# A two-layer convolution and retention decoder on one core: input blocks in the order v, gate, conv, q, k, merge gates, and matmuls kept in written order

## The chip, the cores and the metric

The kernel runs on 1 core of one Trainium2 chip. The metric is the device time of one execution in microseconds (us), as the median of several runs. The core has a matrix engine (TensorE, "PE" in the profile, with its weight loads as "PEld"), a vector engine (VectorE, DVE), an activation engine (ScalarE, ACT), GpSimd (POOL) and SyncE (SP), which issues most of the transfers. Each engine works through its own instructions strictly in order and waits for others by semaphores.

## The reference

Two layers over 256 tokens of 1024 channels, in float32. Cut to what matters:

```python
def hybrid_layer(x, ...):
    h = rmsnorm(x, norm_mix)
    cb, cc, cu, q, k, v, g, ga, gb = jnp.split(h @ w_in, split_points, axis=-1)
    y_conv = (cb * causal_conv3(cc * cu, conv_w)) @ w_conv_out
    o = retention(rotary(q), rotary(k), v)       # 4 heads, decayed scores, then values
    o = (o - mean(o)) * rsqrt(var(o) + EPS) * ret_norm   # per head, over 256 value channels
    y_ret = (silu(g) * o) @ w_ret_out
    x = x + (sigmoid(ga) * y_conv + sigmoid(gb) * y_ret) @ w_o
    h2 = rmsnorm(x, norm_mlp)
    return x + square(relu(h2 @ w_up)) @ w_down

def reference(x, ...):
    for i in range(2):
        x = hybrid_layer(x, ...)
    return rmsnorm(x, norm_final)
```

## The kernel before

Channels lie on the 128 partitions and tokens on the free axis, as 8 tiles of 128 channels by 256 tokens. All weights come as 152 blocks of 1024 input by 256 output channels (1 MB each), read once, in the order of use. A block is loaded by SP into one of three `raw` buffers. `split_block` then makes from it two float32r tiles in one of three `parts` buffers: ACT casts the high part (L99), DVE subtracts to get the low part (L100), each in two instructions of 128x1024. Activations are split the same way. `proj` multiplies one block with 32 matmuls: for each of the 8 input tiles and 2 output halves one of 512 columns (high weights times high and low activations together) and one of 256 columns (low weights). `collect` adds the two sums in PSUM (ACT copy, DVE add).

A layer goes through the 32 blocks of the input projection in the order of `IN_ORDER`, then `yc` times `w_conv_out` (4 blocks), `yr` times `w_ret_out` (4), the merged `mg` times `w_o` (4), then the MLP (16 up, 16 down). The very first block is multiplied straight in float32 (`whole_tokens`), since no split is ready.

Work that doesn't belong to one block is queued with `later(n, fn)`: `fn` is emitted after the matmuls of the n-th block from there, that of the block about to begin being the first. This holds the norm factors (`factors`: Newton steps for `rr`), the rotation tables, the score products (`scores`), the value products (`mix_values`), and the head normalisation in two halves i = 0, 1 of two heads: `head_sums(i)` sums the squares over channels with two matmuls into `var_ps`, DVE writes the variance and ACT its square root to `rm`; `head_out(i)` takes a DVE reciprocal, one Newton step (`newton`: three DVE operations), scales `sg` (gate times values) with four DVE operations and splits it into the parts of `yr`, one operand tile of 128x2x256 per head. `proj([yr])` needs the first head's tile, high and low, for its first matmul.

What is emitted in this order is then ordered on each engine by a scheduler at compile time, except what is pinned with `tc.keep_in_program_order`. The row order that results is fixed when the kernel is built.

For value blocks (`value`), DVE sums each row of 256 value channels, scales the sum to a mean, and GpSimd subtracts it (two instructions of 128x256).

Of the kernel before, what the change touches and what calls it, by code (L numbers as in the profile page):

```python
# [18 lines left out]
P = 128  # L19
# [8 lines left out]
BLK = KT * 2 * P  # L28
FIRST = ((1, 1, 2, 2, 2), (2, 2, 4), (4, 4))
AHEAD = 2  # L30
# [4 lines left out]
IN_ORDER = (  # L35
    [("v", V0 + 256 * i) for i in range(4)]
    + [(n, o + 256 * i) for i in range(4) for n, o in (("cc", 1024), ("cu", 2048), ("cb", 0))]
    + [("q", Q0), ("q", Q0 + 256), ("k", K0), ("k", K0 + 256)]
    + [("g", G0 + 256 * i) for i in range(4)]
    + [("ga", GA0 + 256 * i) for i in range(4)]  # L40
# [8 lines left out]
def trunk_kernel(ctx, tc, px, pos, w, cst, mask, out):  # L49
# [80 lines left out]
    def whole_tokens(xs):  # L130

        ps = ps_main.tile([P, 2, 2, T], F32, tag="mm", name="ps")
        raw = next_block()
        for k in range(KT):
            for j in range(2):
                mm(ps[:, j, 0], xs[:, k, j * P:(j + 1) * P], raw[:, 2 * k:2 * k + 2, :], k == 0, k == KT - 1)
        run_waiting()
        t = t2("sum", "sum", 4)
        nc.scalar.copy(t, ps[:, :, 0, :])
        return t  # L140

# [14 lines left out]
    def mm(o, a, b, start, stop):  # L156
        nc.tensor.matmul(o, lhsT=a, rhs=b, start=start, stop=stop, skip_group_check=True)  # L157

# [70 lines left out]
    def column_sums(o, hi, lo):  # L229

        tc.keep_in_program_order(nc.tensor.matmul(o, lhsT=ones, rhs=hi, start=True, stop=False))
        nc.tensor.matmul(o, lhsT=ones, rhs=lo, start=False, stop=True)

# [52 lines left out]
    nc.vector.memset(eps, EPS)  # L286

    nc.scalar.activation(eps2, eps, AF.Square)
    norm = Norm(gains(0, G_MIX), "mix0")
# [3 lines left out]
    for n in FIRST[0]:  # L293
        c = slice(n_par + k0 * T if k0 else 0, n_par + (k0 + n) * T)
        nc.sync.dma_start(out=px_sb[:, c], in_=px[:, c])
        nc.sync.dma_start(out=begun[0][0][:, 2 * k0:2 * (k0 + n), :], in_=w3[0][:, 2 * k0:2 * (k0 + n), :])
        k0 += n
    for i in range(1, len(FIRST)):
        k0 = 0
        for n in FIRST[i]:  # L300
            nc.sync.dma_start(out=begun[i][0][:, 2 * k0:2 * (k0 + n), :], in_=w3[i][:, 2 * k0:2 * (k0 + n), :])
            k0 += n

    xs = stile("xs")
    for k in range(KT):
        nc.vector.tensor_scalar(
            out=xs[:, k, :], in0=x[:, k, :], scalar1=norm.gain[:, k:k + 1], scalar2=None, op0=ALU.mult
        )
        if k % 2:
            split(xs[:, k - 1:k + 1, :], *norm.act.pair(k // 2))  # L310
    for k in range(0, KT, 2):
        split_block(*begun[1], slice(2 * k, 2 * k + 4))
# [43 lines left out]
    for layer in range(DEPTH):  # L356
# [16 lines left out]
        if layer == 0:  # L373
            def squares():
                for p in range(NPAIR):
                    norm.square(p, in_order=True)
            later(1, squares)
            later(2, norm.fold)
            later(1, late_loads)
            later(4, rotation_tables)  # L380
            later(6, nc.sync.dma_start, mask_sb, mask)

        later(3 if layer == 0 else 2, factors)

        later(12, rotations)

# [19 lines left out]

        def value(h, t):
            mu = small.tile([P, 2], F32, tag="mu", name="mu")
            nc.vector.tensor_reduce(out=mu, in_=t, axis=mybir.AxisListType.X, op=ALU.add)
            nc.vector.tensor_scalar(out=mu, in0=mu, scalar1=1.0 / T, scalar2=None, op0=ALU.mult)  # L410
            for c, o_ in ((0, t[:, 0, :]), (1, v1[:, h, :])):
                nc.gpsimd.tensor_scalar(  # L412
                    out=o_, in0=t[:, c, :], scalar1=mu[:, c:c + 1], scalar2=None, op0=ALU.subtract
                )
            split(t[:, 0, :], v0_parts[:, 0, h, :], v0_parts[:, 1, h, :])

# [92 lines left out]
        for name, _ in IN_ORDER:  # L509
            n = seen[name] = seen.get(name, -1) + 1  # L510
            if name == "v":
                value(n, whole_tokens(xs) if layer == n == 0 else collect(proj_tokens(act[0])))
                continue
            if name == "q" and n == 0:
                qk = stile("qk")
                q_parts = s8.tile([P, 2, HEADS, T], F32R, tag="s8", name="q_parts")
                k0_parts = s4.tile([P, 2, HEADS, P], F32R, tag="s4", name="k0_parts")
            elif name == "g" and n == 0:
                sg = stile("sg")
                sc0_parts = s8.tile([P, 2, HEADS, T], F32R, tag="s8", name="sc0_parts")  # L520
                sc1 = s4.tile([P, HEADS, P], F32, tag="s2", bufs=1, name="sc1")
                for h in range(HEADS):
                    later(1 + h, scores, h)
            elif name == "ga" and n == 0:
                osq = s8.tile([P, 2, HEADS, T], F32R, tag="s8", name="osq")
                for h in range(HEADS):
                    later(1 + h, mix_values, h)
            elif name == "ga" and n == 3:
                rm = s8.tile([P, 2, HEADS, T], F32, tag="s8", name="rm")
                later(2, head_sums, 0)  # L530
                later(3, head_sums, 1)
            elif name == "gb" and n == 2:
                yr = Parts("yr")
                later(1, head_out, 0)
                later(3, head_out, 1)
            ps = proj(act)
# [216 lines left out]
```

## Time and profile before

| | before |
|---|---|
| median of 3 runs | 891.73 us (891.69 to 893.56) |
| the profiled execution | 892.27 us |
| its span, first to last instruction | 890.1 us |
| mean granted TensorE clock | 0.994 |
| busy share PE, DVE, ACT, POOL | 99%, 78%, 57%, 28% |

The span is what the views of the trace show; the execution's own time is 2.17 us longer. The granted clock is the share of TensorE's full 2.4 GHz; 0.50 is its lower level of 1.2 GHz. PE's busy time is counted with modelled ends, so a busy PE is not idle but need not be at its peak.

### The profile page before, as it was taken

The page shows a single profiled execution, that of the slowest core. Times are in us where ns is not written, and L with a number is a line of the kernel's source. Part 1 is how long each engine was busy: PE and PEld are TensorE (multiplying, and loading weights), DVE is VectorE, ACT ScalarE, POOL GpSimd, SP SyncE. Part 2 cuts the span into 40 slices and gives each one's busy share as a digit, 9 for nine tenths or more (in the row PEclk, how much of TensorE's full clock was granted, in tenths as well). Part 3 has the DMA queues.
Part 4 walks back from the last instruction along what each step waited for, and adds up shares of the span by engine and source line. Part 5 has one row for each costly group of instructions (what it writes and reads, how often), then busy time and mean ns, then how long its engine had stood idle before and what let it go on. Part 6 is the DMA issues. An engine that isn't in the chain of part 4 may idle for free.

```text
span 890.1 us, 12685 instructions
## 1 busy us (share of the span) xinstructions
PE 877.3 (99%) x5090; PEld 767.9 (86%) x5090; DVE 695.9 (78%) x785; ACT 505.4 (57%) x700; POOL 251.7 (28%) x170
## 2 busy tenths in 40 slices
PE   8999999999999999999999999999999999999996
PEld 6878888888888888888888888888888888888896
DVE  5989999799977966555588989998996897664451
ACT  6445636675556877444455554566654597764440
POOL 2883353421003322000046324443200323210110
PEclk9999999999999999999999999999999999999998
DMA  9645645444654655555545553555355555555521
GB/s 319 233 141 190 205 159 199 179 159 148 231 188 143 237 193 188 192 192 188 193 179 190 189 190 142 189 190 177 130 215 189 189 180 206 189 200 190 191 75 48
DMA packets 24682, 163.00 MB, mean 183 GB/s; under 512 B 2864, under 2 KB 3504, under 8 KB 5552
## 3 DMA queue, kind: packets, MB, share of 16 engines
q1 hardware_dynamic: 24336, 161.68, 51.3%
q8 instruction: 40, 0.66, 0.3%
q10 hardware_dynamic: 288, 0.52, 0.2%
q14 instruction: 18, 0.15, 0.0%
HBM read 161.14 MB, written 1.05 MB: 182 GB/s over the span
## 4 chain that ended last, share of the span: by engine, by line
PE 92%; POOL 3%; DVE 2%; DMA 1%; ACT 1%; issue 0%; SPq 0%; DVEq 0%; POOLq 0%; ACTq 0%
PE ps L157 89%; PE o_ps L157 1%; DVE parts L100 1%; POOL sum L412 1%; DMA raw<-w 1%; PE sc_ps L157 1%; DMA px_sb<-px 0%; ACT parts L99 0%; POOL v L412 0%; POOL mix_sum L258 0%; POOL red L333 0%; POOL sum L432 0%; DVE o L675 0%; POOL turns L339 0%; DVE rs_a L215 0%
## 5 line engine op out<-in xcount | busy, mean ns | idle before, releaser
L100 DVE TENSOR_TENSOR parts<-raw,parts 128x1024 fp32r<-128x1024 f32 (+1 forms) x304 | 411.2, 1384 | 70.4 <-ACT parts L99 69.5
L99 ACT CAST parts<-raw 128x1024 fp32r<-128x1024 f32 (+1 forms) x304 | 302.4, 1044 | 109.2 <-PE ps L157 78.1
L157 PE MATMUL ps<-mix,parts 128*128 128x512 f32 (+1 forms) x1792 | 323.0, 341 | 2.5 <-DVE parts L100 2.5
L157 PEld LDWEIGHTS ps<-mix,parts 128*128 128x128 f32 x1792 | 275.9, 189 | 44.0 <-DVE parts L100 2.8
L157 PE MATMUL ps<-up,parts 128*128 128x512 f32 (+1 forms) x1088 | 179.4, 326 | 0.0
L157 PE MATMUL ps<-mlp,parts 128*128 128x256 f32 (+1 forms) x1024 | 178.5, 335 | 0.0
L157 PEld LDWEIGHTS ps<-up,parts 128*128 128x128 f32 x1088 | 159.1, 188 | 19.6
L157 PEld LDWEIGHTS ps<-mlp,parts 128*128 128x128 f32 x1024 | 155.4, 188 | 22.4 <-issue 0.4
L210 DVE TENSOR_TENSOR sum<-ps,sum 128x512 f32<-128x512 f32 x87 | 59.4, 683 | 43.7 <-ACT sum L209 43.7
L209 ACT COPY sum<-ps 128x512 f32<-128x512 f32 x87 | 50.6, 582 | 75.2 <-PE ps L157 75.2
L594 POOL TENSOR_TENSOR u<-u,rr2m 128x512 f32<-128x512 f32 x32 | 47.7, 1492 | 123.4 <-ACT u L604 106.1
L258 POOL TENSOR_TENSOR mix_sum<-mix_sum,sq 128x512 f32<-128x512 f32 x8 | 12.6, 1574 | 145.1 <-ACT sq L254 145.1
L258 POOL TENSOR_TENSOR mlp_sum<-mlp_sum,sq 128x512 f32<-128x512 f32 x6 | 12.9, 2158 | 122.7 <-ACT sq L254 122.7
L157 PE MATMUL ps<-yr,parts 128*128 128x512 f32 (+1 forms) x256 | 44.7, 336 | 0.0
L157 PE MATMUL ps<-mg,parts 128*128 128x512 f32 (+1 forms) x256 | 44.7, 336 | 0.0
L157 PE MATMUL ps<-yc,parts 128*128 128x512 f32 (+1 forms) x256 | 44.7, 336 | 0.0
L157 PEld LDWEIGHTS ps<-yc,parts 128*128 128x128 f32 x256 | 39.1, 188 | 5.2
L157 PEld LDWEIGHTS ps<-yr,parts 128*128 128x128 f32 x256 | 39.1, 188 | 5.2
L157 PEld LDWEIGHTS ps<-mg,parts 128*128 128x128 f32 x256 | 39.1, 188 | 5.2
L157 PE MATMUL ps<-parts,mix 128*128 128x512 f32 (+1 forms) x224 | 39.8, 338 | 0.0
L157 PEld LDWEIGHTS ps<-parts,mix 128*128 128x128 f32 x224 | 34.2, 188 | 5.0
L100 DVE TENSOR_TENSOR up<-u,up 128x512 fp32r<-128x512 f32 x32 | 26.1, 820 | 0.0
(175 smaller groups left out, 666.6 us busy)
## 6 DMA issues: line engine op xcount, KB each, us to landing
raw<-w SPq DMA_DIRECT2D x149, 1024.0 KB, 4.8
raw<-w SPq DMA_DIRECT2D x3, 512.0 KB, 7.5
raw<-w SPq DMA_DIRECT2D x5, 256.0 KB, 6.1
px_sb<-px SPq DMA_DIRECT2D x3, 256.0 KB, 4.6
mask_sb<-mask SPq DMA_DIRECT2D x1, 512.0 KB, 7.2
out<-o SPq DMA_DIRECT2D x2, 256.0 KB, 2.3
out<-o ACTq DMA_DIRECT2D x2, 256.0 KB, 2.5
raw<-w SPq DMA_DIRECT2D x2, 128.0 KB, 2.7
```

Of the source, the lines that this page charges most:

```text
L99: nc.scalar.copy(hi, src)
L100: nc.vector.tensor_tensor(out=lo, in0=src, in1=hi.bitcast(F32), op=ALU.subtract)
L157: nc.tensor.matmul(o, lhsT=a, rhs=b, start=start, stop=stop, skip_group_check=True)
L209: nc.scalar.copy(t, ps[:, :, 1, :])
L210: nc.vector.tensor_tensor(out=t, in0=ps[:, :, 0, :], in1=t, op=ALU.add)
L258: nc.gpsimd.tensor_tensor(out=self.sum, in0=self.sum, in1=sq, op=ALU.add)
L412: nc.gpsimd.tensor_scalar(out=o_, in0=t[:, c, :], scalar1=mu[:, c:c + 1], scalar2=None, op0=ALU.subtract)
L594: nc.gpsimd.tensor_tensor(out=u, in0=u, in1=both(rr2), op=ALU.mult)
```

## The change

Six things are changed. The input projection's order becomes v, g, conv (cc, cu, cb), q, k, ga, gb, where the gate blocks g stood between k and ga. The deferred work is hung on other blocks: scores on ga, values on gb, `head_sums` on the first two blocks behind gb, `head_out(0)` and `head_out(1)` on the second and third. Every matmul of `mm` is pinned in written order. The value mean is subtracted by ACT and DVE in place of GpSimd, and DVE takes the row sum along with the addition of the two PSUM halves. The pieces of x are loaded from ACT's queue, in three pieces in place of five, with the first weight block in three pieces too. The squares of the first norm move ahead of the first block, and `factors` one block earlier in layer 0.

```diff
-FIRST = ((1, 1, 2, 2, 2), (2, 2, 4), (4, 4))
+FIRST = ((2, 2, 4), (4, 4), (4, 4))
...
     [("v", V0 + 256 * i) for i in range(4)]
+    + [("g", G0 + 256 * i) for i in range(4)]
     + [(n, o + 256 * i) for i in range(4) for n, o in (("cc", 1024), ("cu", 2048), ("cb", 0))]
     + [("q", Q0), ("q", Q0 + 256), ("k", K0), ("k", K0 + 256)]
-    + [("g", G0 + 256 * i) for i in range(4)]
...
     def mm(o, a, b, start, stop):
-        nc.tensor.matmul(o, lhsT=a, rhs=b, start=start, stop=stop, skip_group_check=True)
+        tc.keep_in_program_order(nc.tensor.matmul(o, lhsT=a, rhs=b, start=start, stop=stop, skip_group_check=True))
...
-        nc.sync.dma_start(out=px_sb[:, c], in_=px[:, c])
+        nc.scalar.dma_start(out=px_sb[:, c], in_=px[:, c])
...
             split(xs[:, k - 1:k + 1, :], *norm.act.pair(k // 2))
+            norm.square(k // 2, in_order=True)
...
-            def squares():
-                for p in range(NPAIR):
-                    norm.square(p, in_order=True)
-            later(1, squares)
-            later(2, norm.fold)
+            later(1, norm.fold)
...
-        later(3 if layer == 0 else 2, factors)
-
-        later(12, rotations)
+        later(2, factors)
+
+        later(16, rotations)
...
-        def value(h, t):
-            mu = small.tile([P, 2], F32, tag="mu", name="mu")
-            nc.vector.tensor_reduce(out=mu, in_=t, axis=mybir.AxisListType.X, op=ALU.add)
-            nc.vector.tensor_scalar(out=mu, in0=mu, scalar1=1.0 / T, scalar2=None, op0=ALU.mult)
-            for c, o_ in ((0, t[:, 0, :]), (1, v1[:, h, :])):
-                nc.gpsimd.tensor_scalar(
-                    out=o_, in0=t[:, c, :], scalar1=mu[:, c:c + 1], scalar2=None, op0=ALU.subtract
-                )
-            split(t[:, 0, :], v0_parts[:, 0, h, :], v0_parts[:, 1, h, :])
+        def value(h, ps, whole):
...
+                nc.scalar.copy(t, ps[:, :, 1, :])
+                for c in range(2):
+                    nc.vector.scalar_tensor_tensor(
+                        out=t[:, c, :], in0=ps[:, c, 0, :], scalar=1.0, in1=t[:, c, :], op0=ALU.mult, op1=ALU.add,
+                        accum_out=mu[:, c:c + 1],
+                    )
+            nc.vector.tensor_scalar(out=mu, in0=mu, scalar1=-1.0 / T, scalar2=None, op0=ALU.mult)
+            hi, lo = v0_parts[:, 0, h, :], v0_parts[:, 1, h, :]
+            nc.scalar.activation(hi, t[:, 0, :], AF.Identity, bias=mu[:, 0:1])
+            nc.vector.scalar_tensor_tensor(
+                out=lo, in0=t[:, 0, :], scalar=mu[:, 0:1], in1=hi.bitcast(F32), op0=ALU.add, op1=ALU.subtract
+            )
+            nc.scalar.activation(v1[:, h, :], t[:, 1, :], AF.Identity, bias=mu[:, 1:2])
...
-            elif name == "ga" and n == 3:
+            elif name == "gb" and n == 3:
                 rm = s8.tile([P, 2, HEADS, T], F32, tag="s8", name="rm")
+                yr = Parts("yr")
                 later(2, head_sums, 0)
                 later(3, head_sums, 1)
-            elif name == "gb" and n == 2:
-                yr = Parts("yr")
-                later(1, head_out, 0)
-                later(3, head_out, 1)
+                later(3, head_out, 0)
+                later(4, head_out, 1)
```

**PE, the head sums.** On PE, before, the first `var_ps` pair (L231, L232) stands behind the first gb block, whose activations are `mix`:

```order
L157 MATMUL ps<-mix_103,parts 128x512
L157 MATMUL ps<-mix_103,parts 128x256
L231 MATMUL var_ps<-osq,ones 128x512
L232 MATMUL var_ps<-osq,ones 128x512
L157 MATMUL ps<-mix_102,parts 128x512
L157 MATMUL ps<-mix_102,parts 128x256
```

In the changed kernel it stands behind the first block with `yc` activations:

```order
L155 MATMUL ps<-yc_177,parts 128x512
L155 MATMUL ps<-yc_177,parts 128x256
L155 MATMUL var_ps<-osq,ones 128x512 x2
L155 MATMUL ps<-yc_176,parts 128x512
L155 MATMUL ps<-yc_176,parts 128x256
```

Between the first `var_ps` and the first matmul that reads `yr` PE had seven blocks; it now has three.

**DVE, the head normalisation.** On DVE, before, the end of this work looked so (`tb` is a collected gb block, `sum` a collected yc block):

```order
L215 TENSOR_TENSOR rs_a<-rm 128x512
L217 SCALAR_TENSOR_TENSOR rm<-rs_a,rm 128x512
L210 TENSOR_TENSOR tb<-ps,tb 128x512
L100 TENSOR_TENSOR parts<-raw,parts 128x1024
L216 SCALAR_TENSOR_TENSOR rs_a<-rs_a,rm 128x512
L100 TENSOR_TENSOR parts<-raw,parts 128x1024
L500 SCALAR_TENSOR_TENSOR sg<-sg,hg,rm 128x256 x4
L217 SCALAR_TENSOR_TENSOR rm<-rs_a,rm 128x512
L210 TENSOR_TENSOR sum<-ps,sum 128x512
L100 TENSOR_TENSOR parts<-raw,parts 128x1024 x2
L100 TENSOR_TENSOR yr_1750<-sg,yr_1750 128x2x256
```

In the changed kernel the work begins with the variance of the first half, behind the first yc block:

```order
L493 TENSOR_SCALAR rm<-var_ps 128x512
L208 TENSOR_TENSOR sum<-ps,sum 128x512
L100 TENSOR_TENSOR parts<-raw,parts 128x1024
L567 SCALAR_TENSOR_TENSOR ta<-ta,sum 128x512
L100 TENSOR_TENSOR parts<-raw,parts 128x1024
L501 RECIPROCAL rm<-rm 128x512
L493 TENSOR_SCALAR rm<-var_ps 128x512
L208 TENSOR_TENSOR sum<-ps,sum 128x512
L100 TENSOR_TENSOR parts<-raw,parts 128x1024
L213 TENSOR_TENSOR rs_a<-rm 128x512
L100 TENSOR_TENSOR parts<-raw,parts 128x1024
L567 SCALAR_TENSOR_TENSOR ta<-ta,sum 128x512
```

Then come the second `RECIPROCAL` and one L214, each of 128x512, and then these rows, up to the first low part of `yr`:

```order
L208 TENSOR_TENSOR sum<-ps,sum 128x512
L100 TENSOR_TENSOR parts<-raw,parts 128x1024 x2
L213 TENSOR_TENSOR rs_a<-rm 128x512
L215 SCALAR_TENSOR_TENSOR rm<-rs_a,rm 128x512
L567 SCALAR_TENSOR_TENSOR ta<-ta,sum 128x512
L208 TENSOR_TENSOR sum<-ps,sum 128x512
L100 TENSOR_TENSOR parts<-raw,parts 128x1024 x2
L214 SCALAR_TENSOR_TENSOR rs_a<-rs_a,rm 128x512
L506 SCALAR_TENSOR_TENSOR sg<-sg,hg,rm 128x256 x4
L567 SCALAR_TENSOR_TENSOR ta<-ta,sum 128x512
L215 SCALAR_TENSOR_TENSOR rm<-rs_a,rm 128x512
L100 TENSOR_TENSOR yr_1760<-sg,yr_1760 128x2x256 x2
```

All four collected yc blocks (L208 `sum`) and the splits of four later weight blocks now stand ahead of the first low part of `yr`; before, only one collected yc block did. The second layer has the same rows.

**ACT, the first gated blocks of layer 0.** On ACT, before, the first convolution scaling (L437 `acc`) stands ahead of two weight casts (`sh` and `turns` are the sines of the rotation tables):

```order
L346 ACT_TABLE_LOAD
L346 ACTIVATE sh<-ang 128x256
L209 COPY sum<-ps 128x512
L99 CAST parts<-raw 128x1024 x2
L349 ACTIVATE turns<-turns 128x256
L437 ACTIVATE acc<-sum,px_sb 128x256 x2
L209 COPY sum<-ps 128x512
L99 CAST parts<-raw 128x1024 x2
```

In the changed kernel the first gate's tanh (L426 `th`) has that place, ahead of the casts of the ninth block of the input projection:

```order
L207 COPY sg<-ps 128x512
L99 CAST parts<-raw 128x1024 x2
L345 ACT_TABLE_LOAD
L345 ACTIVATE sh<-ang 128x256
L348 ACTIVATE turns<-turns 128x256
L426 ACT_TABLE_LOAD
L426 ACTIVATE th<-sg 128x512
L207 COPY sg<-ps 128x512
L99 CAST parts<-raw 128x1024 x2
```

Both sines now stand directly ahead of the tanh, with no block's copy and casts between them.

## Rows read from the trace of the kernel before

**Rows 1.** What PE waited for, whole span: total us, times, longest.

```profile
PE ps L157 <- DVE parts L100: 2.5, 1, 2.5
```

**Rows 2.** Stages: us, busy us and count of each engine, granted clock, DMA share, GB/s.

```profile
67.00:71.00 4.00, 3.96 (x14) 3.44 (x15) 3.18 (x5) 2.25 (x4) 0.16 (x1) 0.57 0.45 147
71.00:72.00 1.00, 1.00 (x8) 0.86 (x7) 1.00 (x2) 0.75 (x1) 1.00 (x1) 1.00 1.03 434
```

**Rows 3.** Timeline, ACT and DVE ahead of PE's wait: start, us, engine, operation.

```profile
60.12 0.91 ACT L437 ACTIVATE acc<-sum,px_sb 128x256 f32<-128x256 f32 x2 [5.71 <-POOL sum L432]
...
61.40 2.00 ACT L99 CAST parts<-raw 128x1024 fp32r<-128x1024 f32 x2
...
64.70 3.41 DVE L100 TENSOR_TENSOR parts<-raw,parts 128x1024 fp32r<-128x1024 f32 x2
```

**Rows 4.** GpSimd's groups from 17 to 65 us: busy us, mean ns.

```profile
L412 POOL TENSOR_SCALAR sum<-sum,mu 128x256 f32<-128x256 f32 x4 | 8.2, 2052 | 14.1 <-DVE mu L410 14.0
L412 POOL TENSOR_SCALAR v<-sum,mu 128x256 f32<-128x256 f32 x4 | 4.8, 1188 | 0.0
```

**Rows 5.** Timeline of PE, first layer, from the head sums to `yr`.

```profile
182.82 0.39 PE L231 MATMUL var_ps<-osq,ones 128*128 128x512 f32 x1
...
183.28 5.81 PE L157 MATMUL ps<-mix,parts 128*128 128x512 f32 x32
188.93 0.40 PE L231 MATMUL var_ps<-osq,ones 128*128 128x512 f32 x1
...
200.50 22.35 PE L157 MATMUL ps<-yc,parts 128*128 128x512 f32 x128
222.69 1.55 PE L157 MATMUL ps<-yr,parts 128*128 128x512 f32 x8
```

**Rows 6.** Timeline of DVE in the same stretch.

```profile
183.48 0.69 DVE L487 TENSOR_SCALAR rm<-var_ps 128x512 f32<-128x512 f32 x1 [0.90 <-PE var_ps L232]
...
187.54 3.35 DVE L495 RECIPROCAL rm<-rm 128x512 f32<-128x512 f32 x1 [0.46 <-ACT rm L490]
190.81 0.63 DVE L487 TENSOR_SCALAR rm<-var_ps 128x512 f32<-128x512 f32 x1
...
200.32 3.44 DVE L100 TENSOR_TENSOR parts<-raw,parts 128x1024 fp32r<-128x1024 f32 x2
...
211.65 0.68 DVE L210 TENSOR_TENSOR sum<-ps,sum 128x512 f32<-128x512 f32 x1
212.25 2.34 DVE L100 TENSOR_TENSOR parts<-raw,parts 128x1024 fp32r<-128x1024 f32 x2
214.52 0.68 DVE L100 TENSOR_TENSOR yr<-sg,yr 128x512 fp32r<-128x512 f32 x1
215.13 1.66 DVE L500 SCALAR_TENSOR_TENSOR sg<-sg,hg,rm 128x256 f32<-128x256 f32 x4
216.71 0.68 DVE L100 TENSOR_TENSOR yr<-sg,yr 128x512 fp32r<-128x512 f32 x1
```

**Rows 7.** Timeline of ACT in the same stretch.

```profile
185.52 1.28 ACT L490 ACT_TABLE_LOAD   x1
186.82 0.69 ACT L490 ACTIVATE rm<-var_ps,eps 128x512 f32<-128x512 f32 x1
```

**Rows 8.** Timeline, second layer, the same place.

```profile
655.81 14.38 PE L157 MATMUL ps<-yr,parts 128*128 128x512 f32 x82
```

**Rows 9.** Stages of the start, columns as in the stages above.

```profile
5.00:8.00 3.00, 2.07 (x8) 1.44 (x8) 1.31 (x3) 0.87 (x2) 0.00 (x0) 1.00 0.89 252
11.00:14.00 3.00, 3.00 (x16) 2.60 (x16) 2.08 (x4) 2.16 (x4) 0.00 (x0) 1.00 1.04 416
```

**Rows 10.** Timeline of the start, PE and DVE.

```profile
9.88 3.69 PE L157 MATMUL ps<-raw,xs 128*128 128x256 f32 x16 [0.32 <-DMA raw<-w]
10.41 0.62 DVE L306 TENSOR_SCALAR xs<-px_sb 128x256 f32<-128x256 f32 x2 [0.24 <-DMA px_sb<-px]
...
13.22 17.00 PE L157 MATMUL ps<-parts,mix 128*128 128x512 f32 x96
```

More of the change, by code (lines that the diff above doesn't have):

```diff
@@ L137, in whole_tokens @@
         run_waiting()
-        t = t2("sum", "sum", 4)
-        nc.scalar.copy(t, ps[:, :, 0, :])
-        return t
+        return ps
     waiting = []
@@ L229, in column_sums @@
     def column_sums(o, hi, lo):
-        tc.keep_in_program_order(nc.tensor.matmul(o, lhsT=ones, rhs=hi, start=True, stop=False))
-        nc.tensor.matmul(o, lhsT=ones, rhs=lo, start=False, stop=True)
+        mm(o, ones, hi, True, False)
+        mm(o, ones, lo, False, True)
     class Norm:
@@ L286, in trunk_kernel @@
     nc.vector.memset(eps, EPS)
-    nc.scalar.activation(eps2, eps, AF.Square)
     norm = Norm(gains(0, G_MIX), "mix0")
@@ L294, in trunk_kernel @@
         c = slice(n_par + k0 * T if k0 else 0, n_par + (k0 + n) * T)
-        nc.sync.dma_start(out=px_sb[:, c], in_=px[:, c])
+        nc.scalar.dma_start(out=px_sb[:, c], in_=px[:, c])
         nc.sync.dma_start(out=begun[0][0][:, 2 * k0:2 * (k0 + n), :], in_=w3[0][:, 2 * k0:2 * (k0 + n), :])
         k0 += n
+    tc.keep_in_program_order(nc.scalar.activation(eps2, eps, AF.Square))
     for i in range(1, len(FIRST)):
@@ L405, in rotate @@
                 split(d[:, :, :P], k0_parts[:, 0, h, :], k0_parts[:, 1, h, :])
-        def value(h, t):
-            mu = small.tile([P, 2], F32, tag="mu", name="mu")
-            nc.vector.tensor_reduce(out=mu, in_=t, axis=mybir.AxisListType.X, op=ALU.add)
-            nc.vector.tensor_scalar(out=mu, in0=mu, scalar1=1.0 / T, scalar2=None, op0=ALU.mult)
-            for c, o_ in ((0, t[:, 0, :]), (1, v1[:, h, :])):
-                nc.gpsimd.tensor_scalar(
-                    out=o_, in0=t[:, c, :], scalar1=mu[:, c:c + 1], scalar2=None, op0=ALU.subtract
-                )
-            split(t[:, 0, :], v0_parts[:, 0, h, :], v0_parts[:, 1, h, :])
+        def value(h, ps, whole):
+            t, mu = t2("sum", "sum", 4), small.tile([P, 2], F32, tag="mu", name="mu")
+            if whole:
+                nc.scalar.copy(t, ps[:, :, 0, :])
+                nc.vector.tensor_reduce(out=mu, in_=t, axis=mybir.AxisListType.X, op=ALU.add)
+            else:
+                nc.scalar.copy(t, ps[:, :, 1, :])
[11 more added lines that the diff above has]
+            nc.scalar.activation(v1[:, h, :], t[:, 1, :], AF.Identity, bias=mu[:, 1:2])
         def gate(p, ps):
@@ L511, in trunk_kernel @@
             if name == "v":
-                value(n, whole_tokens(xs) if layer == n == 0 else collect(proj_tokens(act[0])))
+                whole = layer == n == 0
+                value(n, whole_tokens(xs) if whole else proj_tokens(act[0]), whole)
                 continue
-            if name == "q" and n == 0:
+            if name == "g" and n == 0:
+                sg = stile("sg")
+            elif name == "q" and n == 0:
                 qk = stile("qk")
@@ L517, in trunk_kernel @@
                 k0_parts = s4.tile([P, 2, HEADS, P], F32R, tag="s4", name="k0_parts")
-            elif name == "g" and n == 0:
-                sg = stile("sg")
+            elif name == "ga" and n == 0:
                 sc0_parts = s8.tile([P, 2, HEADS, T], F32R, tag="s8", name="sc0_parts")
@@ L523, in trunk_kernel @@
                     later(1 + h, scores, h)
-            elif name == "ga" and n == 0:
+            elif name == "gb" and n == 0:
                 osq = s8.tile([P, 2, HEADS, T], F32R, tag="s8", name="osq")
```

## The prediction

> **What bounds the kernel now.** I read the page's busy shares first (PE 99%), then who PE waited for, and then, since a busy PE leaves little else, the few places where it did not run. The list of PE's waits has one long entry: 2.5 us for a DVE split of weights [rows 1]. It lies at 64.6 to 67.0 us in the first layer, and it costs more than its length, because the granted clock stands at 0.57 over the next 4 us, part of that at the lower level of 1.2 GHz, and is back at 1.00 in the microsecond behind [rows 2]. 4 x (1 - 0.57) = 1.7 us is lost in that way. So the place costs 2.5 + 1.7 = 4.2 us. From there to the tail PE runs without a wait. A change can therefore win at this place and at the start, and it can lose wherever another engine is made to deliver later than PE asks.
>
> What is behind that wait is a queue, not a busy engine: ACT stood idle for 5.7 us in front of the first convolution scaling, waiting for GpSimd, and only then, at 61.4 us, could it cast the next weights, which DVE took up at 64.7 [rows 3].
>
> **The change part by part.**
>
> *The wait at 67 us.* GpSimd was late there since it had the rotation tables, the factors' products and the value means to do. The means were 8 instructions of 8.2 + 4.8 = 13.0 us [rows 4]; they go, the factors come one block earlier, and the convolution comes later. The first gate's tanh now has the place in ACT's queue that the convolution scaling had: it waits for the sines and for GpSimd's product with `rr`, and behind it stand the casts of the ninth block. That block is due seven blocks behind the second, which begins at 13.2 us [rows 10]; at 5.6 us a block (below) this is 52.4, so the casts must begin by about 50. ACT was let go at 60.1 us [rows 3]; without GpSimd's 13.0 us of means that becomes 47, some 3 us in time. Bounds: the wait goes whole (-4.2), or one of the same price comes at the gate (0). I take -4.2, since more is taken out of the queue that made it (13.0) than it was long.
>
> The new value step gives ACT one short instruction more and DVE one row sum less. PE covers both, as long as the splits come in time; if that cover is gone, the price is the same wait, which the upper bound holds.
>
> *The head normalisation.* This is where I see the loss. PE had seven blocks between the first `var_ps` and the first matmul on `yr`: 182.8 to 222.7, that is 39.9 us [rows 5]. It has three now. A block takes 5.65 us beside a `var_ps` pair (183.28 to 188.93), a pair 0.46 us (182.82 to 183.28), and a block of the undisturbed run (222.69 - 200.50) / 4 = 5.55 us [rows 5]. Counted from the first `var_ps`, PE would be ready for `yr` at 0.46 + 5.65 + 0.46 + 2 x 5.55 = 17.7 us.
>
> DVE must bring the first low part of `yr` by then, and its rows of the changed kernel (shown with the change) say what stands ahead of it. From start to start the trace gives:
> - 0.60 us for an operation of 128x512 (211.65 to 212.25), 16 of them: 9.6 us
> - 2.27 us for two splits of 128x1024 (212.25 to 214.52), 8 splits: 9.1 us
> - 3.27 us for a reciprocal (187.54 to 190.81), two: 6.5 us
> - 1.58 us for the four scalings of `sg` (215.13 to 216.71), one group: 1.6 us
> - 0.68 us for the first low part of `yr` itself
>
> All from [rows 6]. The sum is 27.5 us. DVE begins 0.66 us behind the first `var_ps` (182.82 to 183.48) [rows 5, 6]. So the first `yr` part comes at 28.1 us, and PE waits 28.1 - 17.7 = 10.4 us. ACT does not stretch it: its square root stands behind one table load of 1.28 us and takes 0.69 us [rows 7], behind a copy and two casts; with 0.5 for the copy and 2.0 for the casts it ends at some 4.7 us, when DVE reaches the reciprocal.
>
> DVE's order is fixed, so it can't put the `yr` work ahead: the collection of the fourth yc block and the split for a block that is due only two blocks later both stand in front of it. Before, the first low part of `yr` was made at 214.5 us [rows 6], 8 us ahead of PE's 222.7.
>
> Bounds: were splits to run at the 3.4 us a pair that they take beside GpSimd [rows 6], the four pairs would add 4 x 1.15 = 4.6 us. GpSimd has nothing queued in this stretch (its last gate product and square sum come before), so I take 2.27. Below, if the operations overlap their ends a little better, 1 us less. The matmuls for the third and fourth heads start half a block later, and their parts follow at the same pace; I add nothing for them.
>
> Then the clock. A wait of 2.5 us was followed by 1.7 us of loss [rows 2]; one of 10 us should be followed by one at least like it. Bounds: nothing, and twice 1.7. I take 1.7.
>
> The second layer has the same three blocks and the same DVE rows, and its `yr` matmuls began without a wait [rows 8]. So the loss comes twice: 2 x (10.4 + 1.7) = 24.2 us.
>
> *The start.* The two queues issue at once, and the pieces are larger. Before, the last piece of x was there at 10.4 us and the first split block began at 13.2 [rows 10]. After, the last piece holds four of the eight tiles: from its landing T it takes one scaling (0.3) and 16 passes of four tiles (3.7) [rows 10] until that block can start, at T + 4.0. It gains only if T is below 9.2. The transfers ran at 252 GB/s from 5 to 8 us, and at 416 from 11 to 14, where the pieces were larger [rows 9]. With the 2.15 MB of x and the first block at the old rate, T stays 10.4 and 1.2 us are lost; with half of it at 416, T is 1.7 less, 8.7, and 0.5 us are won; with all of it, T is 7.0 and 2.2 us are won. Bounds: -2.2 and +1.2. I take 0, between the first two: the DMA share was already 0.89 in the slow stage [rows 9], so a second queue has little idle time to fill.
>
> The Trainium skill, "DMA: Bandwidth & Descriptors", section "Issuing engines are not separate DMA queues", says that transfers issued by several engines interleave on the same 16 DMA engines and that only the sequencer's time of initiating them is saved. The busy share above agrees. By that rule the second queue is worth almost nothing and the sum stays; if it were worth the whole step from 252 to 416 GB/s, the sum would be 2.2 us less.
>
> *Written order of the products.* In both kernels the norm's two sums stand among the blocks. They are now behind the second block. They are due at 13.2 + 5.6 = 18.8 us; DVE's work ahead of their low part (the second block's splits, a row sum, half a block's split) is some 5 us that begin near 12. Bounds: 0, and 1 us. I take 0.
>
> **The sum.** 890.1 - 4.2 + 24.2 + 0 = 910.1 us of span. The profiled execution took 892.27 for its 890.1, that is 2.17 more, which gives 912.3; the median of the runs is 0.54 below the profiled execution, so 911.7.
>
> **The rivals.**
> 1. *The head work is hidden after all (faster).* The price is then only the gains: 891.7 - 4.2 = 887.5. It needs DVE to be through with its rows in 17.7 us, 10.4 less than they sum to. The point of decision is plain: the 27.5 us would have to shrink by more than a third. Against it stands that every duration is measured in this place; for it, that DVE had room before, but over seven blocks. 4%.
> 2. *The stall is partly hidden.* If the `yr` parts come 3 to 8 us late in place of 10.4, the time is 891.7 - 4.2 + 2 x (3 to 8 + 1.7) = 897 to 907. It needs DVE operations to run some 10 to 25% closer together than anywhere in the rows. 7%.
> 3. *A new wait at the gates too.* The tanh takes the place of the convolution scaling and the wait at 67 us comes back, earlier; or the norm's pinned sums wait a microsecond. 911.7 + 4.2 = 916, or 917. For it: two table loads and both sines stand directly ahead of that tanh, and the margin above is only 3 us. Against it: everything else in that queue became shorter. 12%.
> 4. *The change brings nothing at either place*, a gain and a loss that cancel: 2%, at 891.7.
> 5. The forecast, 911.7, has 75%; each of its bounds taken alone leaves it between 908 and 915 (start -2.2 or +1.2, clock 0 or 3.4 us for each wait, 1 us less in each).
>
> The range takes in 2 in its upper part and 3: 904 to 919. What two measurements of this kernel can tell apart is about 0.2%, or 1.8 us; by the cases above slower has 0.94, the same 0.02, faster 0.04.
>
> **What would show it.** Right: in the trace of the changed kernel PE has two long waits, both at the first matmul on `yr`, both on DVE, 9 to 12 us each, with a granted clock near 0.5 behind them; DVE has no gap in front of them; the wait at 67 us is gone. Wrong: no wait at `yr`, or one on ACT; a reciprocal that takes much less than 3.3 us; a wait in the gate blocks; a first split block that begins more than 2.2 us away from 13.2 us.

## The result, and the profile after

The changed kernel took 922.67 us (median of 4 runs, 922.04 to 923.48), the kernel before 891.94 beside it. The ratio is 1.0341, with a 95% interval of 1.0323 to 1.0359. The prediction was 911.7 us with a range of 904 to 919: the sign and the main cost were right, the time was 11 us more and lies outside the range. The profiled execution took 922.04 us for a span of 920.3, which is 30.2 more than before.

PE's list of waits (total us, times, longest) answers to [rows 1]:

```profile
PE ps L155 <- DVE yr L100: 20.7, 2, 10.3
PE ps L155 <- DVE mg L100: 2.7, 2, 1.4
PE ps L155 <- DVE xs L304: 2.6, 1, 2.6
PE ps L155 <- DVE mlp L245: 2.0, 2, 1.0
...
PE ps L155 <- DVE mix L245: 0.8, 1, 0.8
```

The 2.5 us for `parts` are gone. Two long waits for `yr` have come, and four kinds of short ones that the prediction had not. The first `yr` wait in PE's timeline (start, us, engine, operation, and the wait ahead of it), against [rows 5]:

```profile
204.61 0.62 PE L155 MATMUL var_ps<-osq,ones 128*128 128x512 f32 x2
205.06 5.81 PE L155 MATMUL ps<-yc,parts 128*128 128x512 f32 x32
210.71 0.64 PE L155 MATMUL var_ps<-osq,ones 128*128 128x512 f32 x2
211.18 11.26 PE L155 MATMUL ps<-yc,parts 128*128 128x512 f32 x64
232.78 7.39 PE L155 MATMUL ps<-yr,parts 128*128 128x512 f32 x29 [10.33 <-DVE yr L100]
```

PE is through with its three blocks 17.8 us behind the first `var_ps` (222.45) and gets the first low part of `yr` 28.2 us behind it. What DVE did meanwhile, against [rows 6]:

```profile
209.34 3.35 DVE L501 RECIPROCAL rm<-rm 128x512 f32<-128x512 f32 x1
...
217.21 3.35 DVE L501 RECIPROCAL rm<-rm 128x512 f32<-128x512 f32 x1
...
225.69 0.69 DVE L208 TENSOR_TENSOR sum<-ps,sum 128x512 f32<-128x512 f32 x1
226.29 2.35 DVE L100 TENSOR_TENSOR parts<-raw,parts 128x1024 fp32r<-128x1024 f32 x2
228.55 0.69 DVE L214 SCALAR_TENSOR_TENSOR rs_a<-rs_a,rm 128x512 f32<-128x512 f32 x1
229.15 1.67 DVE L506 SCALAR_TENSOR_TENSOR sg<-sg,hg,rm 128x256 f32<-128x256 f32 x4
...
231.94 1.29 DVE L100 TENSOR_TENSOR yr<-sg,yr 128x512 fp32r<-128x512 f32 x2
```

No row here has a wait in brackets: DVE is busy without a gap, in the order and at the prices that the prediction summed. Behind the wait PE is slow. Stages of PE (length, busy us and count, granted clock, DMA share, GB/s), against [rows 2]:

```profile
232.00:234.00 2.00, 1.22 (x4) 0.50 0.37 143
234.00:236.00 2.00, 2.00 (x8) 0.50 0.00 0
236.00:238.00 2.00, 2.00 (x10) 0.71 0.00 0
238.00:240.00 2.00, 2.00 (x13) 1.00 0.00 0
```

8 matmuls start in 2 us at the lower level of 1.2 GHz, 13 at 2.4. The second layer, and two of the short waits (PE's timeline):

```profile
681.18 24.25 PE L155 MATMUL ps<-yr,parts 128*128 128x512 f32 x128 [10.32 <-DVE yr L100]
...
711.04 18.63 PE L155 MATMUL ps<-mg,parts 128*128 128x512 f32 x104 [1.36 <-DVE mg L100]
...
734.87 5.38 PE L155 MATMUL ps<-mlp,parts 128*128 128x512 f32 x28 [0.95 <-DVE mlp L245]
```

And the start, against [rows 10]:

```profile
6.47 9.84 PE L155 MATMUL ps<-raw,xs 128*128 128x256 f32 x32 [2.55 <-DVE xs L304]
16.41 2.97 PE L155 MATMUL ps<-parts,mix 128*128 128x512 f32 x15
```

The first split block begins at 16.41 us; before it was 13.22.

The account of the span: yr waits 10.33 + 10.32 = 20.65; the clock behind them, by the 128 `yr` matmuls of 24.83 us (all of them together) and 24.25 against 22.35 for the 128 yc ones of [rows 5], 2.5 + 1.9 = 4.4; start 16.41 - 13.22 = 3.2; short waits 2.7 + 2.0 + 0.8 = 5.5; the wait at 67 us and its clock -4.2. That is 29.6 of the 30.2.

### The profile page after: what moved, and what is told of

It reads as the page before. It is cut to its first block, busy times and chain, and to the rows that moved or that the text cites. A ratio compares the mean times of both kernels' runs of the same rounds, so it can differ in the third digit from the quotient of the medians.

```text
span 920.3 us, 12662 instructions
## 1 busy us (share of the span) xinstructions
PE 882.5 (96%) x5090; PEld 771.4 (84%) x5090; DVE 700.0 (76%) x799; ACT 504.6 (55%) x702; POOL 211.6 (23%) x154
## 4 chain that ended last, share of the span: by engine, by line
PE 88%; DVE 8%; issue 2%; DMA 1%; ACT 0%; ACTq 0%; DVEq 0%
PE ps L155 87%; DVE parts L100 3%; PE o_ps L155 1%; DMA px_sb<-px 1%; DVE sum L208 1%; DVE rm L501 1%; DVE ta L567 1%; PE sc_ps L155 1%; DVE sg L506 0%; DVE mlp L245 0%; DVE rs_a L213 0%; DVE rs_a L214 0%; DVE rm L215 0%; DVE o L682 0%; DVE rm L493 0%
## 5 line engine op out<-in xcount | busy, mean ns | idle before, releaser
L155 PE MATMUL ps<-mix,parts 128*128 128x512 f32 (+1 forms) x1792 | 318.1, 339 | 0.0
L155 PE MATMUL ps<-mlp,parts 128*128 128x512 f32 (+1 forms) x1024 | 179.2, 336 | 2.0 <-DVE mlp L245 2.0
L207 ACT COPY sum<-ps 128x512 f32<-128x512 f32 x80 | 46.9, 586 | 124.5 <-PE ps L155 124.5
L208 DVE TENSOR_TENSOR sum<-ps,sum 128x512 f32<-128x512 f32 x80 | 55.0, 687 | 68.4 <-ACT sum L207 68.3
L155 PE MATMUL ps<-yr,parts 128*128 128x512 f32 (+1 forms) x256 | 49.1, 357 | 20.7 <-DVE yr L100 20.7
L155 PEld LDWEIGHTS ps<-yr,parts 128*128 128x128 f32 x256 | 42.0, 202 | 27.7 <-issue 21.2
L256 POOL TENSOR_TENSOR mlp_sum<-mlp_sum,sq 128x512 f32<-128x512 f32 x6 | 8.0, 1334 | 158.5 <-ACT sq L252 158.5
L155 PE MATMUL ps<-parts,mix 128*128 128x512 f32 x224 | 40.5, 340 | 0.9 <-DVE mix L245 0.8
```

The source lines that it names most:

```text
L155: tc.keep_in_program_order(nc.tensor.matmul(o, lhsT=a, rhs=b, start=start, stop=stop, skip_group_check=True))
L207: nc.scalar.copy(t, ps[:, :, 1, :])
L208: nc.vector.tensor_tensor(out=t, in0=ps[:, :, 0, :], in1=t, op=ALU.add)
L256: nc.gpsimd.tensor_tensor(out=self.sum, in0=self.sum, in1=sq, op=ALU.add)
```

## The experiments

Fourteen kernels, each timed beside the kernel before (medians of 891.7 to 891.9 us). Ratio and 95% interval are against the kernel before.

| run | base and edit | us | ratio |
|---|---|---|---|
| e1 | changed, old order and hooks | 895.4 | 1.0037 (1.0024 to 1.0049) |
| e2 | changed, products not pinned | 918.97 | 1.0312 (1.0294 to 1.0330) |
| e3 | changed, old loads of x | 919.36 | 1.0305 (1.0291 to 1.0319) |
| e4 | changed, no reciprocal | 907.32 | 1.0176 (1.0162 to 1.0190) |
| f1 | before, early squares | 889.81 | 0.9976 (0.9965 to 0.9988) |
| f2 | before, new loads of x | 892.0 | 0.9997 (0.9988 to 1.0006) |
| f3 | before, products pinned | 902.25 | 1.0119 (1.0104 to 1.0135) |
| f4 | before, new value step | 885.62 | 0.9933 (0.9920 to 0.9945) |
| g1 | f4, new order | 916.15 | 1.0272 (1.0258 to 1.0286) |
| g2 | changed, yc collected later | 916.76 | 1.0282 (1.0265 to 1.0299) |
| g3 | changed, head work earlier | 916.61 | 1.0277 (1.0263 to 1.0291) |
| g4 | g1, head work earlier | 906.57 | 1.0166 (1.0152 to 1.0180) |
| h1 | f4, early squares | 888.42 | 0.9959 (0.9945 to 0.9973) |
| h2 | f4, new loads of x | 889.46 | 0.9970 (0.9959 to 0.9982) |

**e1, the order undone; g1, the order alone.** In e1 the g blocks go back behind k, and the scores, the values, `head_sums` and `head_out` to their old hooks; g1 makes that part of the change on top of the value step.

```diff
-    + [("g", G0 + 256 * i) for i in range(4)]
     + [(n, o + 256 * i) for i in range(4) for n, o in (("cc", 1024), ("cu", 2048), ("cb", 0))]
     + [("q", Q0), ("q", Q0 + 256), ("k", K0), ("k", K0 + 256)]
+    + [("g", G0 + 256 * i) for i in range(4)]
```

> The changed kernel with the order of before for the input blocks and its hooks (the first gate behind k, head sums and head work seven blocks ahead of the first matmul on yr); the pin, the new start and the new value step stay. Theory A (DVE's queue in front of the first yr part against a room of three blocks): both waits at yr and the low clock behind them go, 922.7 - 2 x (10.3 + 2.2) = 897.7 us, and what is left over the kernel before is the start (+3.2) and the waits of the pin (+5.5), less the wait at 67 us (-4.2). Theory B (the pin alone makes the yr wait, since PE may not go past a late yr block): the waits at yr stay with the pin, some 920 us.

> The kernel before with the new value step and the new order with its hooks, and nothing else of the change (loads, squares and free products as before); the run with the value step alone took 885.6 us. Theory A (room of three blocks against DVE's queue): two waits at yr of 10.3 us each with a low clock behind them, 885.6 + 2 x (10.3 + 2.2) = 910.6 us. Theory B (the waits at yr need the pin or the start too): waits under 5 us, below 900 us.

e1 gave back 27.3 us, and no wait for `yr` is left in it; the 3.5 us that it keeps over the kernel before are the start (3.2) and the pin's short waits (5.6) less the wait at 67 us (4.2), to 1.1 us. g1 has both, 10.3 us each as in the changed kernel, with free products and the old start. Its span is 29.1 us over that of f4: 20.7 of yr waits, 2.9 of four waits at mlp, and 5.0 of the clock behind the yr waits (24.26 and 25.43 us for 128 yr matmuls against 22.35). As its first split block begins 2.2 us earlier than f4's (13.10 against 15.27), 2.7 us stay unaccounted for. Theory A holds: the order with its hooks is enough for the long waits, and nothing else of the change is needed. The price was set too low, at 25 against 30.5 by the medians.

**e2, the pin undone; f3, the pin alone.** e2 takes `keep_in_program_order` out of `mm` (and gives the column sums their form of before), f3 puts it into the kernel before.

```diff
-        tc.keep_in_program_order(nc.tensor.matmul(o, lhsT=a, rhs=b, start=start, stop=stop, skip_group_check=True))
+        nc.tensor.matmul(o, lhsT=a, rhs=b, start=start, stop=stop, skip_group_check=True)
```

> The changed kernel with the products free of the pin, as before (the first product of the column sums alone is held in order). Theory A: the yr waits stay at 10 us each, since everything that PE has left then stands behind yr; only the waits at mg, mlp and mix go (1.37 + 1.36 + 1.03 + 0.95 + 0.81 = 5.5 us): 922.7 - 5.5 = 917.2 us. Theory B (the pin made the yr waits): they shrink by more than half and the time is under 908 us. Theory C (the pin costs nothing, the five waits come from the later blocks' other order): 922 us.

> The kernel before with one edit: all products in written order. If the pin makes the five waits at mg, mlp and mix by itself: 891.9 + 5.5 = 897.4 us, and the wait at 67 us as before. If what the free order saves is partly given back as other waits (the run without the pin had four waits at mlp, 2.9 us together, that the kernel before has not): some 894 us. If it costs nothing: 892 us.

PE's waits in e2:

```profile
PE ps L155 <- DVE yr L100: 20.6, 2, 10.3
PE ps L155 <- DVE mlp L245: 2.9, 4, 0.9
```

The long waits stay at 10.3 us, so the pin does not make them. mg and mix are gone, but mlp grew from 2.0 to 2.9. So 2.6 us of short waits went, not 5.5; by the medians 3.7 us came back. g1 has the same 2.9 us at mlp with free products too: that part comes with the new order, and without the pin. PE's waits in f3:

```profile
PE mix_st L157 <- ACT mix_sh L99: 5.4, 1, 5.4
PE ps L157 <- DVE mg L100: 2.9, 2, 1.4
PE ps L157 <- DVE mlp L247: 2.0, 2, 1.0
...
PE mix_st L157 <- DVE mix_sl L100: 1.0, 1, 1.0
PE ps L157 <- DVE mix L247: 0.8, 1, 0.8
```

The same waits at mg, mlp and mix, 5.7 us, in a kernel without a wait for `yr`: in the old order these are the pin's own. Before, PE's products of two or three blocks stood interleaved around the late operand; now they stand behind it. It shows in ACT's copies of the first three MLP blocks' sums: they begin at 279.09, 282.00 and 284.89 us before, where three blocks end close together, and at 279.95, 285.50 and 291.29 in f3, a whole block apart. f3 lost 10.4 us in all, more than any theory said, because the norm's two sums (`mix_st`) now hold PE too, for 6.4 us, with a granted clock of 0.50 from 32 to 36 us behind them. In the changed kernel the early squares have them ready by 22.2 us, and they cost nothing. (The wait at 67 us, expected to stay in f3, is gone as well: PE comes there later.)

**e3, f1, f2, h1, h2: the start.** e3 puts the loads back:

```diff
-FIRST = ((2, 2, 4), (4, 4), (4, 4))
+FIRST = ((1, 1, 2, 2, 2), (2, 2, 4), (4, 4))
...
-        nc.scalar.dma_start(out=px_sb[:, c], in_=px[:, c])
+        nc.sync.dma_start(out=px_sb[:, c], in_=px[:, c])
```

> The changed kernel with the x loads on the queue and in the pieces of before; the early sums of squares stay. If the start's 3.2 us come from the load (queue and pieces): first split block back at 13.2 us, 922.7 - 3.2 = 919.5 us. If they come from the squares moved into the scalings on GpSimd and DVE: the first split block stays at 16.4 us, time 922.

The time came back as expected, but not for the reason given: the first split block of e3 still begins at 16.18 us, now behind a wait of 2.0 us for DVE's parts. So the squares delay it too, and the 3.3 us are no measure of the loads: e3 ran its first layer in the quicker of two rhythms (last section), which is worth some 2 us. f2 makes the opposite edit in the kernel before; f1 moves the squares there:

```diff
             split(xs[:, k - 1:k + 1, :], *norm.act.pair(k // 2))
+            norm.square(k // 2, in_order=True)
...
-            def squares():
-                for p in range(NPAIR):
-                    norm.square(p, in_order=True)
-            later(1, squares)
-            later(2, norm.fold)
+            later(1, norm.fold)
```

> The kernel before with one edit: the squares of x for the norm are made between the scalings of x, as in the changed kernel, instead of one block later. Theory S (the early squares delay the start: GpSimd's work beside DVE stretches the scalings and the first splits): the first split block begins at about 16.2 us with a wait of some 2 us on DVE's parts, followed by a low clock; 891.9 + 3 to 4.5 = 895 to 896.5 us. Theory L (the start's loss comes from the loads alone): first split block at 13.2 us, 892 us.

> The kernel before with one edit: x in the larger pieces and on ACT's queue, the squares as before. Theory L (the loads delay it: the first x lands later, PE idles at the start and its clock rises later): first matmul at 6.5 us in place of 3.8, weight loads of 327 ns until about 12 us, the first split block at 16 us; 894.8 us. Theory S (only the squares): first split block at 13.2 us, 892 us.

Both edits delay the first split block, by 3.4 us the squares alone (16.66) and by 1.8 the loads alone (15.04); together they make 3.2. That the one waits out the other is a reading, and the 1.8 is unsure, for f4 came as late as 15.27 us with the old loads (below). PE in f1, then DVE, then GpSimd:

```profile
13.25 1.99 PE L157 MATMUL ps<-raw,xs 128*128 128x256 f32 x8 [1.01 <-DVE xs L306]
16.66 7.56 PE L157 MATMUL ps<-parts,mix 128*128 128x512 f32 x41 [1.41 <-DVE parts L100]
```

```profile
11.75 1.71 DVE L306 TENSOR_SCALAR xs<-px_sb 128x256 f32<-128x256 f32 x2
```

```profile
11.78 1.27 POOL L258 TENSOR_TENSOR mix_sum<-mix_sum,sq 128x512 f32<-128x512 f32 x1 [1.74 <-ACT sq L254]
```

Two scalings take 1.71 us while GpSimd adds squares; in [rows 10] two took 0.62. Yet f1 did not become slower, and f2 stayed the same: neither has the wait at 67 us any more. Two readings were open, and two more runs were made to tell them apart, with each edit on top of the value step, which has no such wait.

> The kernel before with the value step and the early squares. The early squares alone brought the first split block from 13.2 to 16.7 us and yet no loss (889.8). Theory absorbed (GpSimd's chain sets a date near 67 us, at which PE waits anyhow, so a start up to 4 us later is free there; without that wait it counts in full): against the value step alone (885.6) 3 us are lost, 888.5 to 889.5 us. Theory relief (early squares take work from GpSimd's chain and have a gain of their own): 885 us or less.

> The kernel before with the value step and the new loads of x. The new loads alone brought the first split block from 13.2 to 15.0 us and no loss (892.0). Theory absorbed: without the wait at 67 us the later start counts, 885.6 + 1 to 2 = 886.5 to 887.5 us. Rival (the loads cost nothing in themselves, or give back later what they take): 885.6 us.

Against f4, 2.8 and 3.8 us are lost, where theory absorbed had 3 and 1 to 2: the sign fits it, and the second size does not. That the later start is the cause is not shown, since in the profiled executions h1 and h2 began their first split block only 1.0 and 0.5 us later than f4 (16.26 and 15.73 against 15.27), and f4 ran its first layer in the quicker rhythm. What the traces of f1 and f2 do show is the other half: PE comes to the place at 67 us later, and finds no wait. The spans of runs in the same rhythm agree better: f1 stands at 889.4 us, 3.4 - 4.2 = -0.8 being due and -0.7 found; f2 at 889.1, where 1.8 - 4.2 + 1.1 (two new waits at the scores) = -1.3 was due and -1.0 found; and h1 at 889.4 like f1, as if the value step brought nothing once a late start has taken the wait away (by the medians h1 is 1.4 us under f1, which is within the rhythm). The rows of f1 fit this. Its first convolution scaling on ACT:

```profile
60.59 0.91 ACT L434 ACTIVATE acc<-sum,px_sb 128x256 f32<-128x256 f32 x2 [7.01 <-POOL sum L429]
```

That is no earlier than the 60.12 of [rows 3], so ACT was let go no sooner; PE comes 3.4 us later. (DVE works in another order there: the first half of the split is made from 63.32 to 65.35 us, 1.6 earlier than before, which alone would not have done for a PE that comes at 64.6.)

**f4, the value step alone.**

```diff
-                nc.gpsimd.tensor_scalar(
-                    out=o_, in0=t[:, c, :], scalar1=mu[:, c:c + 1], scalar2=None, op0=ALU.subtract
-                )
...
+            nc.scalar.activation(hi, t[:, 0, :], AF.Identity, bias=mu[:, 0:1])
+            nc.vector.scalar_tensor_tensor(
+                out=lo, in0=t[:, 0, :], scalar=mu[:, 0:1], in1=hi.bitcast(F32), op0=ALU.add, op1=ALU.subtract
+            )
```

> The kernel before with one edit: the value means off GpSimd (on DVE, with ACT's Identity), order and start as before. If GpSimd's 13 us of value work made the wait at 67 us: the wait of 2.5 us and the low clock behind it go, 891.9 - 4.2 = 887.7 us. Rival (the new order is needed for it, ACT stays held by the rotation tables and the factors): the wait stays, 891.9 us.

This is the version that beats both kernels, 6.2 us under the kernel before. Its first convolution scaling on ACT:

```profile
56.78 0.91 ACT L446 ACTIVATE acc<-sum,px_sb 128x256 f32<-128x256 f32 x2 [5.09 <-POOL sum L441]
```

It comes 3.3 us earlier, more than PE waited, and the wait at 67 us is gone. This execution also started late, though nothing was changed there. PE at the start, and the stage from 8 to 12 us (PE busy and count, granted clock, DMA share, GB/s):

```profile
8.52 7.11 PE L155 MATMUL ps<-raw,xs 128*128 128x256 f32 x24 [1.65 <-DMA raw<-w]
15.27 8.90 PE L155 MATMUL ps<-parts,mix 128*128 128x512 f32 x49
```

```profile
8.00:12.00 4.00, 3.48 (x9) 0.58 1.01 373
```

PE waited 1.65 us for weights, the clock fell, and the first split block came 2.1 us later than before. So, as in f1, a later PE could have missed the wait. But here the splits are earlier too. The first half of the split that PE had waited for (64.70 in [rows 3], ready for PE at 67.04):

```profile
59.51 2.03 DVE L100 TENSOR_TENSOR parts<-raw,parts 128x1024 fp32r<-128x1024 f32 x1
```

It ends at 61.5 us (the second half at 64.4), ahead of the 64.6 at which PE came to it in the kernel before, so the wait would be gone with the old start too. Of the 6.2 us, 4.2 are that wait and its clock; 2 are of the size of the rhythm.

**e4, g2, g3, g4: DVE's queue and the room.** e4 leaves out the reciprocal in `head_out`; g2 pins the addition that collects a yc block behind the head work; g3 and g4 call the head work earlier:

```diff
-            nc.vector.reciprocal(rs, rs)
```

```diff
-            t = collect(proj([yc]))
+            ps, t = proj([yc]), t2("sum", "sum", 4)
+            nc.scalar.copy(t, ps[:, :, 1, :])
+            tc.keep_in_program_order(
+                nc.vector.tensor_tensor(out=t, in0=ps[:, :, 0, :], in1=t, op=ALU.add)
+            )
```

```diff
-            elif name == "gb" and n == 3:
+            elif name == "gb" and n == 1:
...
-                later(3, head_sums, 1)
                 later(3, head_out, 0)
-                later(4, head_out, 1)
+                later(4, head_sums, 1)
+                later(5, head_out, 1)
```

> The changed kernel without the reciprocal ahead of the head scaling (it leaves out 1/x of the root, 3.35 us of DVE for each half; the later scaling then takes the root itself). Theory A: each yr wait shrinks by at least the two reciprocals' worth less what DVE does in another order, to some 3.5 us: 906 to 909 us, the low clock behind the wait smaller too. Rival (PE waits for something else that stands in DVE's place, the square root or a collected block): the wait stays above 8 us, 920 us.

> The changed kernel with one edit: the addition that collects a yc block keeps its written place on DVE, and so stands behind the head work that is called ahead of it; the work is the same. Theory A (what stands in DVE's queue ahead of the first yr part sets the wait): the rows ahead of the first yr part sum to 25.7 us in place of 28.1, so the wait is about 8 us, 922.7 - 2 x 2.3 = 918 us. Rival (the chain from the sums over the root to the scaling sets it, not the queue): the wait stays at 10.3 us, 922 us.

PE in e4:

```profile
219.86 2.94 PE L155 MATMUL ps<-yr,parts 128*128 128x512 f32 x16
226.90 3.35 PE L155 MATMUL ps<-yr,parts 128*128 128x512 f32 x9 [4.09 <-DVE yr L100]
```

The first half's parts now come in time, and PE waits 4.1 us for the second half's: 8.2 in both layers in place of 20.7, and 15.4 us less time. In g2 the waits are 8.1 us each where the rows summed to 8. So the queue of rows ahead of the part sets the wait, row by row. (g2's time fell by 5.9, not 4.6; in e4 and g2 both layers ran in the quicker rhythm, which is part of what they gained.)

> The changed kernel with one edit: the sums and the head work of heads 0 and 1 two blocks earlier, those of heads 2 and 3 one block earlier; the order of the input blocks and all else stay. Theory A (it is the room between the sums and the first yr block): the first half has five blocks of room, the second half four, some 8.3 us of DVE's rows leave the stretch: waits at yr of 0 to 3 us, 922.7 - 2 x (7.3 to 10.3 + 2.2) = 898 to 904 us. Rival (DVE is full in the gate blocks too, so the work only pushes weight splits late): a wait of like size on parts in the merge gates, 915 us or more.

> The kernel before with the new value step, the new order, and the head work early as in the run before this one; loads, squares and free products as before. If only the place of the head work is wrong with the new order, this comes to that of the value step alone, 885.6 us, plus what is left of the waits at yr (0 to 3 us each): 885 to 892 us. If the new order costs something else too: above 895 us.

Here theory A's numbers failed. PE in g3, then DVE ahead of the second sum:

```profile
204.91 0.50 PE L155 MATMUL var_ps<-osq,ones 128*128 128x512 f32 x1 [2.06 <-DVE osq L100]
...
223.45 2.94 PE L155 MATMUL ps<-yr,parts 128*128 128x512 f32 x16
231.02 4.21 PE L155 MATMUL ps<-yr,parts 128*128 128x512 f32 x12 [4.64 <-DVE yr L100]
```

```profile
196.06 3.35 DVE L501 RECIPROCAL rm<-rm 128x512 f32<-128x512 f32 x1 [0.42 <-ACT rm L496]
199.33 0.63 DVE L208 TENSOR_TENSOR tb<-ps,tb 128x512 f32<-128x512 f32 x1
199.88 3.44 DVE L100 TENSOR_TENSOR parts<-raw,parts 128x1024 fp32r<-128x1024 f32 x2
...
204.44 0.41 DVE L100 TENSOR_TENSOR osq<-osq 128x256 fp32r<-128x256 f32 x1
```

The first half is in time, but its reciprocal and a slow pair of splits now stand ahead of the last `osq` part, which holds the second `var_ps` for 2.06 us, and the second half is still 4.6 us late. The rival was right in kind (the work pushes something else late) and wrong in place (the sum, not the weight splits). g4 lost 21 us to f4: waits of 7.6 us at mg and 4.8 at yr, and a low clock behind them (0.70 from 228 to 232 us, 0.50 from 247.3 to 250). With the hooks that were tried, the new order thus leaves too little room: in g3 DVE is busy without a gap from 200 to 220 us, and PE still waits. Whether another hook would do was not tried.

## Why the prediction was wrong

- **The wait at 67 us**: right. -4.2 predicted; it is gone, and f4 shows that the value step alone takes it away. That a PE that comes later finds no wait there either (f1 and f2) was not seen. No new wait came at the gates (rival 3).
- **The head normalisation**: right, with its mechanism. 10.4 us predicted for each layer, 10.33 and 10.32 measured; g1 shows the order as the cause, e4 and g2 the queue.
- **The clock after it**: 1.7 each predicted, 2.5 and 1.9 measured, within the bounds.
- **The start**: mis-sized, with half of it left out. "I take 0", between -2.2 and +1.2; it is +3.2, beyond the 2.2 us that the prediction had set as a sign of being wrong. The sum spoke of the loads alone. Of these its worse bound was near: the last piece of x was scaled from 10.32 us (10.59 in f2), no earlier than before, and f2's first split block came at 15.04, 0.4 behind T + 4.0, with a PE that ran slowly until about 10 us (weight loads of 334 ns from 8 to 10, 203 from 10 to 12; see the last section). The squares, moved into the same stretch, were not costed at all, and alone they make 3.4. The rule that the prediction weighed (the Trainium skill, "DMA: Bandwidth & Descriptors", section "Issuing engines are not separate DMA queues": a second issuing engine saves only the time of initiating) agrees with the trace in the end, not on the way: from 5 to 8 us the transfers ran at 403 GB/s, where [rows 9] have 252, but the last x was no earlier. So the DMA share of 0.89 did not mean that there was little room, as the prediction took it. Queue and piece size were changed together, and that the weight pieces shared the rate was not tried by itself.
- **Written order of the products**: this is the step that failed. "Bounds: 0, and 1 us. I take 0" looked only at the norm's two sums, which indeed cost nothing. Every other product is pinned too. The sum had no term for what comes behind `yr`, and there the three places at mg, mlp and mix take 5.7 us in f3 by the pin alone, and 5.5 in the changed kernel. Of those 5.5 the pin has 2.6 to itself; 2.9 at mlp come with the new order also where the products are free (e2, g1), and what makes them stays open. The place to look was PE's order before: at mg and mlp products of several blocks stood interleaved, and there the free order was covering a late operand.

With start and short waits in place of the two zeros the sum is 911.7 + 3.2 + 5.5 = 920.4; the clock's further 1.0 makes 921.4, against 922.7.

## What to carry to other kernels

Before products are pinned to their written order, look where a free order has interleaved blocks: such a place may cover a late operand, and the cover is lost there, not only at the lines that the edit names. When deferred work is moved towards its reader, sum the rows that stand ahead of it in the queue of its engine against the time of the blocks left; that sum held to 0.1 us here. Sum the rows at the new place too: in g3 they made another operand late. A delay ahead of a wait that another engine dates can be free, as in f1 and f2. It can then cost its price once another edit has taken that wait away: the account of the changed kernel needs the start's 3.2 us and the 4.2 of the wait as separate terms.

## What was not expected of the hardware

**The clock at the start.** The page gives a granted clock of 1.00 from the start, but PE's weight loads in the changed kernel (groups of 8 to 10 us, of 12 to 14, and of 234 to 236, where the clock reads 0.50; count, busy us, mean ns) say otherwise:

```profile
L155 PEld LDWEIGHTS ps<-raw,xs 128*128 128x128 f32 x5 | 1.7, 337 | 0.4
...
L155 PEld LDWEIGHTS ps<-raw,xs 128*128 128x128 f32 x11 | 2.2, 198 | 0.3
...
L155 PEld LDWEIGHTS ps<-yr,parts 128*128 128x128 f32 x7 | 2.0, 330 | 0.4
```

At 8 to 10 us a load takes as long as at a clock of 0.50. In the kernel before it took 189 ns in the same two microseconds. PE, idle for 2.55 us between its warming matmuls and the first block, came to full speed later, and the clock column did not show it. In f4 the column does show such a stretch: 0.50 from 10 to 12 us, with weight loads of 322 ns.

**Two rhythms at one clock.** In the input blocks of a layer, PE kept one of two paces, both with a granted clock of 1.00, and which one differed from run to run and from layer to layer. Stages of weight loads in f4 (first layer, second layer), then in h1:

```profile
80.00:100.00 20.00, 17.62 (x117) 1.00 0.62 214
480.00:500.00 20.00, 17.32 (x114) 1.00 0.56 194
```

```profile
80.00:100.00 20.00, 17.32 (x115) 1.00 0.58 206
480.00:500.00 20.00, 17.33 (x115) 1.00 0.54 197
```

117 loads in 20 us against 114 or 115 is 2% or more. From the first split block to the first yc block of the first layer f4 took 180.8 us (15.27 to 196.10) and h1, with the same blocks in the same order, 183.3 (16.26 to 199.53): 2.4 us. It blurs every difference of that size between the runs above; what chooses the pace stays open.
